# One decoder step on one core: prompt projections normalised in groups of four token tiles, rope tables built one stage earlier, and the two page loads of a quad issued apart

## Chip, cores and metric

The kernel runs on one core of one Trainium2 chip. The metric is device time in microseconds (us) from one launch to its end; the median of several executions is compared. A profile of one execution is used to see where the time goes.

Engines are named as the profile names them: PE (TensorE matmuls), PEld (its weight loads, which overlap the matmuls), DVE (VectorE), ACT (ScalarE), POOL (GpSimd) and SP (SyncE, whose queue issues nearly all DMAs here).

## The reference, cut to what matters

One decoder layer for two groups of requests with the same weights: a prompt of 1024 tokens and eight samples of four new tokens, each sample with 4096 past tokens kept in pages. The three sub-layers are a mixer, a cross-attention into 256 memory tokens and a gated ConvFFN. The mixer is what the change touches:

```
u, v, cq, ckv, kpe = split_in(rms_norm(x) @ w_in)        # 1024 -> 512 | 512 | 256 | 256 | 32
a_out = chunk_gmlp(u, v, ...)                            # group A, 512 wide
ckv_n = rms_norm(ckv)
q = qk_rope(rms_norm((rms_norm(cq) @ w_uq) as 8 heads x 96))
k = qk_rope(rms_norm(concat(ckv_n @ w_uk as 8 x 64, kpe broadcast to 8 heads x 32)))
v = ckv_n @ w_uv
b_out = causal softmax attention of q, k, v              # group B, 512 wide
mixed = concat(rms_norm(a_out), rms_norm(b_out)) @ w_o
```

For the samples the keys and values of the past are computed from the paged latents (`cache_ckv`, 256 wide) and un-rotated rope keys (`cache_kpe`, 32 wide) that `page_table` names. The RMS norm of each key head runs over its 64 projected and its 32 rope columns, and the rope half is rotated by position after the norm.

## The kernel before, in words

All matmuls work on float32 split into a high and a low part: `mm3` (line 179, its matmuls have line 185) issues three products for each pair of operands. Tokens are cut into nine tiles: eight of 128 prompt tokens and one of the 32 sample tokens. Outside the stretches named below a planner (`tc`, with a cost model) orders the instructions of every engine; inside `tc.manual_schedule(engines=...)` the named engines keep the order of the program text.

**Latents' stage** (end of `phase1`, lines 485 to 568). After u, v and the gMLP, the latents cq and ckv are projected in three chunks of up to 384 tokens. For each chunk ACT squares, PE sums over partitions, DVE computes the inverse root (`rsqrt_steps`, 11 small DVE instructions, lines 222 to 236) at high priority, and the normalised ckv is written out and split. Between the chunks `mix_group` (lines 1494 to 1522) normalises the group-A outputs in groups of two tiles (five groups), transposes them on PE (line 1519), copies them from PSUM on DVE (line 1520) and stores each tile with one DMA (line 1522) to a DRAM scratch `mix`.

**Prompt projections, first half of the heads** (`phase2a`, lines 597 to 650). Three small tables are loaded; POOL multiplies the cosines and sines with the rope gains for q and for k (`rope_tables`, line 591), squares and rotates the rope keys of all tiles (`kss`, `kr`). Then `proj_group` (line 797) runs for tiles in groups (0,2), (2,4), (4,6), (6,8) and (8,9). A group allocates its buffers (`k` and `q`, rings of four, two tiles each), projects q and k of each tile with copies and squares on ACT and a reduction on DVE (line 828), then calls `norm`: three small DVE instructions (lines 833 to 835), the 11 of the inverse root, one more (line 841), the rope of q on POOL (`rope_tok`, lines 579 to 582), and the scaling of k on DVE (line 850) and of the rope keys on POOL (line 851). The values follow. After the groups `head_prep` transposes q and k of head 0 (line 874) and the first scores begin.

**Heads** (lines 681 to 750). PE, ACT, DVE and POOL are in manual order: 32 units (head, group of two query tiles) in 80 steps of a counter `t`. Work of the second half of the heads is put on chosen steps by `spread`: the four prompt groups of `proj_group` on steps 16 to 20, 18 to 23, 21 to 26 and 24 to 29 (line 672), their values on 28 to 38. On POOL, sums of later weights (`weight_sums`, lines 772 to 776) run on every fourth step. When the outputs of a group of query tiles are complete, a `mix` (line 697) normalises them as above.

**Page loop** (`phase2b`, lines 1050 to 1164). Eight samples with 32 pages each; four pages make a quad, so there are 64 quads, and a step `n` of the loop scores two pages: 128 steps, two for a quad. For quad R two tiles are loaded, with four DMAs each: `cT` (the pages with the features on partitions, latents and rope keys: what the key scores are made from; ring of three, line 1220) and `ck` (the pages with the tokens on partitions, for the values and the sums of squares of the rope keys; ring of 15, line 1224). `quad_load` (line 1202) first brings four page numbers into registers of SP (line 1207: one TENSOR_LOAD and four register computations with range checks), then issues the DMAs. The first three `cT` are loaded during the heads (line 1043), their `ck` at steps -6, -4 and -2; from step 0 on each even step n calls `quad_load` once, for both tiles of quad n/2 + 3 (line 1121). `cT` of quad R is free for quad R + 3 when `quad_prep` has split it (POOL and DVE, line 1252, at step 2R - 1). At step 2R - 3 POOL rotates the rope keys of R (`quad_rot`, lines 1237 to 1239), at step 2R - 1 PE multiplies them (line 1267), and at 2R the scores proper start. `ck` of quad R is read at step 2R + 1 (ACT, line 1260) and by the value matmuls (line 1367) some 20 steps later. PE, ACT, DVE and POOL are in manual order; SP is the planner's, with a dependency (line 1211) that holds its register loads near the DMAs of five quads before. Other tiles pass through the ring of `ck` as well: the last prompt mix, four loads of mixed rows (line 1088, steps 20, 36, 52 and 68) and the first loads of the next stage (line 1130, from step 122).

**After the loop**: memory keys and values (`mem_kv`), output projection, memory attention, the FFN. The change does not touch these.

Of the kernel before, what the change touches and what calls it, by code (L numbers as in the profile page):

```python
# [5 lines left out]
F32 = mybir.dt.float32  # L6
# [148 lines left out]
class Net:  # L155
# [132 lines left out]
    def phase1(self):  # L288
# [198 lines left out]
        def mix(i0):  # L487
            hl = self.t(pl, [P, 2, 4, P], F32, "hl")
            hl = [hl[:, i] for i in range(2)]
            self.mix_group(pl, pp, 0, i0, min(i0 + 2, 9), lambda i: a_all[:, i], hl, lambda j: self.t(pl, [P, 512], F32, "csq", 4), ("st", 3))  # L490
# [17 lines left out]
        ck_tok = self.t(pl, [P, 9], F32, "ck_tok")  # L508
        raws = pl, [P, 512], F32, "uraw", 1
# [6 lines left out]
        for c, (o, n) in enumerate(CH):  # L516
# [50 lines left out]
            for i0 in ((0, 2), (4, 6), (8,))[c]:  # L567
                mix(i0)
# [15 lines left out]
    def rope_tables(self, p, cos, sin, g, name):  # L584

        nc = self.nc
        out = []
        for nm, t in (("c", cos), ("s", sin)):
            o = p[nm] if isinstance(p, dict) else self.t(p, [P, 9, 2, 16], F32, f"{name}_{nm}")
            for h in range(2):  # L590
                nc.gpsimd.tensor_tensor(
                    o[:, :, h], t, g[:, h * 16 : h * 16 + 16].unsqueeze(1).broadcast_to([P, 9, 16]), ALU.mult
                )
            out.append(o.rearrange("p i h d -> p i (h d)"))
        return out

    def phase2a(self):
# [3 lines left out]
        self.kr = self.t(p, [P, 9, 32], F32, "kr")  # L601
# [7 lines left out]
        pre = self.t(px, [P, 1024], F32, "pre", 2)  # L609
        cos, sin = (pre[:, a : a + 144].rearrange("p (i d) -> p i d", i=9) for a in (0, 144))  # L610
        grow = pre[:, 288:352]
        nc.sync.dma_start(cos, I["c_cos"])
        nc.sync.dma_start(sin, I["c_sin"])
        nc.sync.dma_start(grow, I["rows"][:, 1024:].partition_broadcast(P))
        qt = self.rope_tables(p, cos, sin, grow[:, :32], "tq")
        pre2 = self.t(px, [P, 1024], F32, "pre", 2)
        pre2 = {n: pre2[:, a : a + 288].rearrange("p (i h d) -> p i h d", i=9, h=2) for n, a in (("c", 0), ("s", 288))}
        kt = self.rope_tables(pre2, cos, sin, grow[:, 32:], "tk")
        cmraw = pre[:, 640:768]
# [13 lines left out]
        kss = self.t(p, [P, 9], F32, "kss")  # L633
        ksq = pre[:, 352:640].rearrange("p (i d) -> p i d", i=9)
        nc.gpsimd.tensor_tensor(ksq[:, :8], self.kpe[:, :8], self.kpe[:, :8], ALU.mult)
        nc.gpsimd.tensor_tensor(ksq[:NS, 8:], self.kpe[:NS, 8:], self.kpe[:NS, 8:], ALU.mult)
        nc.vector.tensor_reduce(kss[:, :8], ksq[:, :8], AX.X, ALU.add)
        nc.vector.tensor_reduce(kss[:NS, 8:], ksq[:NS, 8:], AX.X, ALU.add)
        for w, i0, i1 in ((P, 0, 8), (NS, 8, 9)):
            k4 = [x[:w, i0:i1].unsqueeze(2) for x in (self.kr, self.kpe)]  # L640
            self.rope_tok(p, k4[0], k4[1], [t[:w, i0:i1] for t in kt], 1, w, i1 - i0)

        rq = self.t(p, [P, 8, 8], F32, "rq")
        c = {"ggq": ggq, "cmask": cmask, "rq": rq, "kss": kss, "qt": qt}
# [30 lines left out]
        spread(sum([v for _, v in late], []) + late[4][0], 28, 38)  # L675
# [5 lines left out]
        with tc.manual_schedule(engines={E.PE, E.Activation, E.DVE, E.Pool}):  # L681
# [13 lines left out]
            hls = []  # L695

            def mix(G):
                yield
                if not hls:
                    hl = self.t(p, [P, 8, 4, 64], F32, "v", 2).rearrange("p a b c -> p (a b c)")  # L700
                    hls.extend(hl[:, a : a + 1024].rearrange("p (k n) -> p k n", k=4) for a in (1024, 0))
                hl = hls.pop()
                hl = [hl[:, :, a : a + P] for a in (0, P)]
                nt = lambda j: self.t(p, [P, 2, 4, 96], F32, "k", 4).rearrange("p m h d -> p (m h d)")[:, :512]
                for k, _ in enumerate(self.mix_steps(pm, pp, 1, 2 * G, 2 * G + 2, lambda i: self.b_all[G][:, i % 2], hl, nt, ("tp", 4))):
                    yield
                    if k:
                        yield

            mixes = {28: 0, 29: 2, 30: 1}  # L710
            wsums = dict(zip(range(22, 75, 4), (NK, NK + 1, *range(NK))))
            self.lows = []
            for n, u in enumerate(units):
                nu = units[n + 2] if n + 2 < len(units) else None
                k = u["n"]
                for j in range(k):
                    self.flush()
                    u["T"](j)
                    for f in outs:
                        f()  # L720
                        done += 1
                        if done in mixes:
                            steps.append(mix(mixes[done]))
# [73 lines left out]
    def proj_group(self, p, pp, hf, i0, i1, s, c, tt=("tp", 4)):  # L797
# [5 lines left out]
        def alloc():  # L803
            nonlocal r, kk, q
            r = self.t(p, [P, 2, 2, 4], F32, "hr", 2)[:tn, :m]
            kk = self.t(p, [P, 2, 4, 96], F32, "k", 4)[:tn, :m] if i0 < 8 else None
            q = self.t(p, [P, 2, 4, 96], F32, "q", 4)[:tn, :m] if i0 < 8 else self.qs[:, hf * 4 : hf * 4 + 4].unsqueeze(1)
# [22 lines left out]
        def norm():  # L830
# [14 lines left out]
            self.rope_tok(p, q[:, :, :, 64:], q[:, :, :, 64:], [t[:tn, i0:i1] for t in c["qt"]], 4, tn, m)  # L845
# [100 lines left out]
    def sample_prep(self, pp):  # L946
# [67 lines left out]
        nc.tensor.transpose(tp, self.kr[:NS, 8], self.ident[:NS, :NS])  # L1014
# [35 lines left out]
    def phase2b(self):  # L1050
# [27 lines left out]
        hl = self.t(p, [P, 4, 288], F32, "ck", 15).rearrange("p k n -> p (k n)")[:, :1024].rearrange("p (m k n) -> p m k n", m=2, k=4)  # L1078
        hl = [hl[:, i] for i in range(2)]
        mix = self.mix_steps(pa, ppt, 1, 6, 8, lambda i: self.b_last[:, i % 2], hl, None, ("m", 1))  # L1080
# [73 lines left out]
        with tc.manual_schedule(engines={E.PE, E.Activation, E.DVE, E.Pool}):  # L1154
            steps(-10, last + 1)
# [46 lines left out]
    def quad_load(self, p, Q, d=None):  # L1202
# [8 lines left out]
        if len(self.page_dma) >= 5:  # L1211
# [286 lines left out]
    def mix_steps(self, p, pp, z, i0, i1, src, hl, nt, tt):  # L1498
# [3 lines left out]
        r = self.t(p, [P, 2], F32, "mixr", 2)[:tn, :m]  # L1502
        ns = []
        for i in range(i0, i1):

            n = nt(i - i0)[:tn] if nt else src(i)[:tn]
            ns.append(n)
            o = n if nt else hl[i - i0][:tn].rearrange("p k n -> p (k n)")
            nc.scalar.activation(o, src(i)[:tn], AF.Square, accum_out=r[:, i - i0 : i - i0 + 1])
# [3 lines left out]
        for i, n in enumerate(ns):  # L1513
            nc.scalar.activation(n, src(i0 + i)[:tn], AF.Copy, scale=r[:, i : i + 1])
# [794 lines left out]
```

## Time and profile before

| | us |
|---|---|
| median of 3 runs | 1870.41 (1868.35 to 1872.27) |
| the profiled execution | 1873.17 |
| its span, first to last instruction | 1871.5 |
| PE busy in the span | 1812.4 (97%) |
| mean granted TensorE clock | 0.991 of full speed |

Stages of the profiled execution, read from the order of the instructions: latents and all before them to 185.3 us, prompt projections (first half) to 221.6, heads to 433.9, page loop to 886.2, the rest to 1871.5.

How to read it: a row of the windows view gives, for one stretch, its length and the busy time of PE, PEld, DVE, ACT and POOL with instruction counts, then the granted clock (1.00 is full speed, 0.50 half), the DMA share and GB/s. A row of the timeline or of a group gives start, duration, engine, line and operation; in square brackets stands how long the engine was idle before it and what ended that. "SPq" is SP's DMA queue: its rows are issues, not transfers.

### The profile page before, as it was taken

How to read it: one execution, taken by the hardware profiler on the slowest of the kernel's cores; microseconds unless marked ns; L12 is line 12 of the kernel's file. 1: busy time of each engine (PE TensorE's matmuls, PEld its weight loads, DVE VectorE, ACT ScalarE, POOL GpSimd, SP SyncE). 2: the span in 40 equal slices, each digit the busy share in tenths (PEclk: the TensorE clock that was granted, in tenths of full speed). 3: DMA queues.
4: the chain of work that ended last, by engine and by line, in shares of the span. 5: the costliest groups of instructions: out<-in, count | busy, mean ns of one | idle time of the engine just before them, and what ended most of it. 6: DMA issues, size and time to landing. Idle time of an engine off the chain costs nothing.

```text
span 1871.5 us, 39806 instructions
## 1 busy us (share of the span) xinstructions
PE 1812.4 (97%) x14402; PEld 1746.4 (93%) x14402; DVE 1382.2 (74%) x2883; ACT 928.9 (50%) x1965; POOL 708.0 (38%) x826
## 2 busy tenths in 40 slices
PE   6999899989999999999999999999999999999999
PEld 6999799889999999998799988899999999999999
DVE  6865967766887667776744676888888888878664
ACT  6435676666555655555533455633333333344442
POOL 1221515643535454443313110267776677500000
PEclk9999899999999999999999999999999999999999
DMA  8202204666776667564554345422222222495242
GB/s 286 70 10 68 82 1 165 222 230 175 219 205 186 180 173 200 162 186 128 182 157 134 135 158 154 129 67 81 81 82 90 69 72 77 113 352 167 78 154 76
DMA packets 139784, 260.18 MB, mean 139 GB/s; under 512 B 20546, under 2 KB 82851, under 8 KB 136515
## 3 DMA queue, kind: packets, MB, share of 16 engines
q1 hardware_dynamic: 138722, 256.58, 43.8%
q8 instruction: 114, 1.87, 0.4%
q10 hardware_dynamic: 864, 1.05, 0.2%
q14 instruction: 84, 0.68, 0.1%
HBM read 212.27 MB, written 45.30 MB: 138 GB/s over the span
## 4 chain that ended last, share of the span: by engine, by line
PE 61%; issue 5%; SPq 3%; DMA 3%; DVE 3%; POOL 2%; ACT 1%; POOLq 0%; DVEq 0%; ACTq 0%
PE d L185 12%; PE s L185 11%; PE b L185 7%; PE F L185 7%; PE X L185 6%; PE E L185 6%; PE A L185 3%; PE y L185 3%; DMA cT<-cT 2%; SPq L1220 2%; SPq L1224 1%; PE o L1367 1%; PE t L185 1%; POOL cl L1252 1%; PE v L185 1%
## 5 line engine op out<-in xcount | busy, mean ns | idle before, releaser
L185 PE MATMUL s<-w2h,ch 128*128 128x288 f32 (+1 forms) x1024 | 303.7, 297 | 0.0
L185 PE MATMUL s<-w2h,cl 128*128 128x288 f32 (+1 forms) x1024 | 296.0, 289 | 4.2 <-POOL cl L1252 3.0
L185 PE MATMUL s<-w2l,ch 128*128 128x288 f32 (+1 forms) x1024 | 294.6, 288 | 0.0
L185 PEld LDWEIGHTS s<-w2h,ch 128*128 128x128 f32 x1024 | 192.6, 188 | 8.3 <-ACT sq L1292 2.5
L185 PEld LDWEIGHTS s<-w2h,cl 128*128 128x128 f32 x1024 | 192.4, 188 | 6.5 <-POOL cl L1252 5.0
L185 PEld LDWEIGHTS s<-w2l,ch 128*128 128x128 f32 x1024 | 192.8, 188 | 0.0
L1295 DVE TENSOR_REDUCE ss<-sq 128x16 f32<-128x1024 f32 x128 | 155.3, 1213 | 32.4 <-ACT sq L1292 32.2
L1252 POOL TENSOR_TENSOR cl<-cT,ch 128x512 fp32r<-128x512 f32 x64 | 83.7, 1307 | 113.2 <-ACT ch L1248 92.5
L1292 ACT ACTIVATE sq<-s 128x512 f32<-128x512 f32 x128 | 76.6, 598 | 88.8 <-PE s L185 88.7
L1289 ACT ACTIVATE sq<-s 128x512 f32<-128x512 f32 x128 | 76.7, 600 | 74.5 <-PE s L185 74.0
L191 ACT CAST a<-brb 128x528 fp32r<-128x528 f32 x77 | 48.8, 634 | 111.4 <-PE d L185 107.9
L185 PE MATMUL mm<-whi,xh 128*128 128x256 f32 (+3 forms) x288 | 83.4, 291 | 16.4 <-ACT xh L195 10.0
L192 DVE TENSOR_TENSOR a<-brb,a 128x528 fp32r<-128x528 f32 x77 | 54.3, 707 | 58.3 <-ACT a L191 58.3
L185 PE MATMUL d<-a,w 128*128 128x264 f32 x768 | 95.4, 284 | 0.5 <-DVE G L2087 0.5
L185 PEld LDWEIGHTS d<-a,w 128*128 128x128 f32 x768 | 94.3, 188 | 0.7 <-issue 0.7
L932 PEld LDWEIGHTS o<-v,pth 128*128 128x128 f32 x576 | 75.7, 197 | 8.4 <-ACT pth L922 4.2
L185 PE MATMUL mm<-wlo,xh 128*128 128x256 f32 (+3 forms) x288 | 82.1, 288 | 0.0
L185 PE MATMUL mm<-whi,xl 128*128 128x256 f32 (+3 forms) x288 | 82.1, 289 | 0.0
L932 PE MATMUL o<-v,pth 128*128 128x64 f32 x576 | 76.3, 274 | 5.6 <-ACT pth L922 3.3
L1958 POOL TENSOR_TENSOR lo<-s,hi 128x1024 fp32r<-128x1024 f32 x20 | 62.9, 3142 | 45.7 <-ACT hi L1957 45.7
L1248 ACT CAST ch<-cT 128x512 fp32r<-128x512 f32 x128 | 73.4, 625 | 3.7 <-DMA cT<-cT 3.6
L2013 ACT COPY a<-A 128x264 f32<-128x264 f32 x43 | 16.1, 375 | 118.7 <-PE A L185 113.9
(725 smaller groups left out, 6447.5 us busy)
## 6 DMA issues: line engine op xcount, KB each, us to landing
cT<-cT SPq DMA_DIRECT2D x256, 160.0 KB, 2.8
ck<-ck SPq DMA_DIRECT2D x256, 144.0 KB, 3.4
raw<-w_up SPq DMA_DIRECT2D x44, 512.0 KB, 3.6
wsumd<-wsum SPq DMA_DIRECT2D x13, 1024.0 KB, 4.2
actd<-cv SPq DMA_DIRECT2D x44, 264.0 KB, 2.4
brb<-actd SPq DMA_DIRECT2D x44, 264.0 KB, 5.6
wsum<-w_down SPq DMA_DIRECT2D x11, 1024.0 KB, 5.0
raw<-wsumd SPq DMA_DIRECT2D x20, 512.0 KB, 3.7
```

Of the source, the lines that this page charges most:

```text
L185: self.nc.tensor.matmul(out, l, r, start=first and i == 0, stop=last and i == len(seq) - 1)
L191: {"act": nc.scalar.copy, "pool": nc.gpsimd.tensor_copy, "dve": nc.vector.tensor_copy}[eng](hi, src)
L192: low = lambda: nc.vector.tensor_tensor(lo, src, hi, ALU.subtract)
L932: nc.tensor.matmul(u["o"][:, e], th[:, z * P : z * P + P], s["v"][:, jj, h % 4], start=j == z == 0, stop=e == 1 and jj == 2 * G + 1)
L1220: dmas.append([nc.sync.dma_start(cT[:, j], I["cT"][bass.ds(rv, 1)].rearrange("a p n -> (a p) n")) for j, rv in enumerate(rvs)])
L1224: nc.sync.dma_start(ck[j * 32 : j * 32 + 32], I["ck"][bass.ds(rv, 1)].rearrange("a t s f -> (a t) s f"))
L1248: nc.scalar.copy(d["h"][:, k], src[k])
L1252: (nc.vector if k else nc.gpsimd).tensor_tensor(d["l"][:, k], src[k], d["h"][:, k], ALU.subtract)
L1289: nc.scalar.activation(sq[:, 0], ps[:, :, n0 : n0 + 256], AF.Square)
L1292: nc.scalar.activation(sq[:, 1], pt.rearrange("p (e d) -> p e d", e=2), AF.Square)
L1295: yield lambda: nc.vector.tensor_reduce(s["ss"][:, g0 : g0 + 2].rearrange("p e (z h) -> p z e h", z=2), sq.rearrange("p z e (h d) -> p z e ...
L1958: eng.tensor_tensor(lo, src, hi, ALU.subtract)
```

## The change

1. `mix_steps` works on groups of up to four tiles in the latents' stage ((0,4), (4,8), (8,9); the last two are both placed after the second chunk, none after the third). It normalises in place, puts two tiles side by side in one buffer and stores them with one DMA.
2. The rope tables of q, the squares `kss` and the rotated keys `kr` are made in the latents' stage (`rope_setup`, new) instead of at the start of `phase2a`: three DMAs, 16 POOL and 2 DVE instructions there, in place of 18 POOL and 2 DVE instructions.
3. `proj_group` runs for groups (0,4), (4,8), (8,9), with buffers of four tiles in rings of two. In the first half the parts of the groups are interleaved by hand; in the second half the two prompt groups go to steps 16 to 23 and 21 to 29. The rope of four tiles is done two tiles at a time.
4. The prompt mixes in the heads use a buffer of the `k` or `q` ring and have one more step between their two tiles.
5. In the page loop SP joins the manual order. On even steps `quad_load` is called twice: for `cT` of quad n/2 + 3, then for `ck` of quad n/2 + 2. The `ck` of quads 0, 1 and 2 are issued at steps -6, 0 and 1. The dependency of line 1211 is kept for the first three quads alone.

```diff
-            for i0 in ((0, 2), (4, 6), (8,))[c]:
+            for i0 in ((0,), (4, 8), ())[c]:
                 mix(i0)
...
+        self.rope_setup(pl, lat)
...
-        groups = ((0, 2), (2, 4), (4, 6), (6, 8), (8, 9))
-        for g in groups:
-            for f in sum(self.proj_group(p, pp, 0, *g, st[0], c, ("mm", 5)), []):
-                f()
+        groups = ((0, 4), (4, 8), (8, 9))
+        gs = [self.proj_group(p, pp, 0, *g, st[0], c, ("mm", 5)) for g in groups]
+        (qk, v), (qk1, v1), (qk2, _) = gs
+        for f in qk + v + qk1[:5] + v1[:2] + qk1[5:9] + qk2[:3] + qk1[9:] + v1[2:] + qk2[3:]:
+            f()
...
-        for (q, _), t in zip(late, ((16, 20), (18, 23), (21, 26), (24, 29))):
+        for (q, _), t in zip(late, ((16, 23), (21, 29))):
             spread(q, *t)
...
-            kk = self.t(p, [P, 2, 4, 96], F32, "k", 4)[:tn, :m] if i0 < 8 else None
+            kk = self.t(p, [P, 4, 4, 96], F32, "k", 2) if i0 < 8 else None
...
-                if n % 2 == 0 and 0 <= Q + AHEAD < NB * 8:
-                    quads[Q + AHEAD] = self.quad_load(p, Q + AHEAD, quads.get(Q + AHEAD))
+                if n == -6:
+                    self.quad_load(p, 0, quads[0])
+                if n >= 0 and n % 2 == 0 and Q + AHEAD < NB * 8:
+                    quads[Q + AHEAD] = self.quad_load(None, Q + AHEAD)
+                if n == 0:
+                    self.quad_load(p, 1, quads[1])
+                if (n == 1 or n > 0 and n % 2 == 0) and Q + 2 < NB * 8:
+                    self.quad_load(p, Q + 2, quads[Q + 2])
...
-        with tc.manual_schedule(engines={E.PE, E.Activation, E.DVE, E.Pool}):
+        with tc.manual_schedule(engines={E.PE, E.Activation, E.DVE, E.Pool, E.SP}):
             steps(-10, last + 1)
...
-        if len(self.page_dma) >= 5:
+        if p is None and new and len(self.page_dma) >= 5 and Q < 3:
...
         for i, n in enumerate(ns):
+            if i % 2 == 0:
+                hl, w = new(i // 2), min(2, m - i) * tn
             tp = self.t(pp, [P, 512], F32, *tt).rearrange("p (k n) -> p k n", k=4)[:, :, :tn]
             for k in range(4):
                 nc.tensor.transpose(tp[:, k], n[:, k * P : k * P + P], self.ident[:tn, :tn])
-            nc.vector.tensor_copy(hl[i][:, :, :tn], tp)
-            o = t0 + i * tn
-            nc.sync.dma_start(self.mix_dram[:, z * 4 : z * 4 + 4, o : o + tn], hl[i][:, :, :tn])
-            if nt is None and i < m - 1:
+            nc.vector.tensor_copy(hl[:, :, i % 2 * tn : i % 2 * tn + tn], tp)
+            if i % 2 or i == m - 1:
+                o = t0 + i // 2 * 2 * tn
+                nc.sync.dma_start(self.mix_dram[:, z * 4 : z * 4 + 4, o : o + w], hl[:, :, :w])
+            elif z:
                 yield
```

The new function, without its loads:

```python
    def rope_setup(self, p, lat):
        ...
        for nm, t in (("c", cos), ("s", sin)):
            o = self.t(lat, [P, 9, 2, 16], F32, f"tq_{nm}")
            for h in range(2):
                nc.gpsimd.tensor_tensor(o[:, :, h], t, grow[:, h * 16 : h * 16 + 16].unsqueeze(1).broadcast_to([P, 9, 16]), ALU.mult)
        ...
        for w, i0, i1 in ((P, 0, 8), (NS, 8, 9)):
            m = i1 - i0
            x, kr = (y[:w, i0:i1] for y in (self.kpe, self.kr))
            sq = self.t(p, [P, 512], F32, "csq", 4)[:w, : m * 32].rearrange("p (i d) -> p i d", i=m)
            nc.gpsimd.tensor_tensor(sq, x, x, ALU.mult)
            nc.vector.tensor_reduce(self.kss[:w, i0:i1], sq, AX.X, ALU.add)
            nc.gpsimd.tensor_tensor(kr, x, grow[:w, 32:].unsqueeze(1).broadcast_to([w, m, 32]), ALU.mult)
            ...
            for z, y in enumerate((cos, sin)):
                nc.gpsimd.tensor_tensor(t[:, z], ...)
            nc.gpsimd.tensor_tensor(kr[:, :, :16], t[:, 0, :, 0], t[:, 1, :, 1], ALU.subtract)
            nc.gpsimd.tensor_tensor(kr[:, :, 16:], t[:, 0, :, 1], t[:, 1, :, 0], ALU.add)
```

More of the change, by code (lines that the diff above doesn't have):

```diff
@@ L608, in phase2a @@
         st = [{**heads(), **self.wqv}]
[L609 to L619, printed above, removed]
+        cmraw = self.t(px, [P, P], F32, "cmraw")
         nc.sync.dma_start(cmraw, I["c_causal"])
@@ L693, in sample, with mix @@
                 yield from self.pages_ahead()
-            hls = []
-            def mix(G):
+            def mix(G, ring):
                 yield
[L699 to L705, printed above, removed]
+                n = self.t(p, [P, 4, 4, 96], F32, ring, 2).rearrange("p m h d -> p (m h d)")
+                hl = n[:, 512:].rearrange("p (k n) -> p k n", k=4)
+                for k, _ in enumerate(self.mix_steps(
+                    pm, pp, 1, 2 * G, 2 * G + 2, lambda i: self.b_all[G][:, i % 2], lambda j: hl, lambda j: n[:, :512], ("tp", 4)
+                )):
                     yield
```

79 lines of the change are left out of this document (42 added, 37 removed).

## The prediction

> **What bounds the kernel now.** I read the stage table first (the windows view cut at the order of the instructions), because the busy share of the page (PE 97%) is an average.
>
> ```profile
> PE 1812.4 (97%) x14402; PEld 1746.4 (93%) x14402; DVE 1382.2 (74%) x2883; ACT 928.9 (50%) x1965; POOL 708.0 (38%) x826
> ```
> ```profile
> 0.00:185.30 185.30, 168.87 (x1257) 164.73 (x1258) 124.00 (x407) 89.80 (x187) 37.94 (x50) 0.99 0.32 107
> 185.30:221.60 36.30, 28.05 (x203) 25.95 (x203) 35.17 (x128) 24.99 (x122) 24.34 (x47) 0.94 0.39 119
> 221.60:433.90 212.30, 201.01 (x1486) 188.45 (x1485) 147.22 (x510) 144.08 (x385) 86.59 (x92) 0.95 0.40 142
> 433.90:886.20 452.30, 446.98 (x3700) 422.10 (x3702) 335.43 (x641) 261.13 (x572) 209.04 (x339) 1.00 0.65 184
> 886.20:1871.50 985.30, 967.50 (x7766) 945.15 (x7763) 740.39 (x1202) 408.85 (x702) 350.10 (x299) 1.00 0.38 124
> ```
>
> The reader is to see that PE is the bound in all stages but one. In the prompt projections (185.3 to 221.6) it is busy 28.05 of 36.30 us, idle 8.25, and DVE is busy 35.17: there DVE ends last. In the page loop PE is idle 5.3 of 452.3 us: nothing can be won there, only lost. Next, the clock in shorter windows, and PE's timeline at the end of the projections:
>
> ```profile
> 217.60:221.30 3.70, 0.55 (x4) 0.12 (x1) 3.70 (x21) 1.27 (x2) 1.13 (x1) 0.50 0.01 2
> 221.30:227.80 6.50, 6.21 (x21) 5.18 (x22) 5.96 (x25) 2.66 (x7) 0.00 (x0) 0.50 0.00 0
> 309.80:316.60 6.80, 6.76 (x29) 6.73 (x30) 3.23 (x11) 0.95 (x2) 6.41 (x7) 0.50 0.55 230
> ```
> ```profile
> 210.09 0.28 PE L185 MATMUL mm<-wvh,ckh 128*128 128x256 f32 x1
> ...
> 213.13 0.28 PE L185 MATMUL mm<-w2h,ckl 128*32 128x256 f32 x1
> ...
> 216.91 1.25 PE L874 MATMUL tp<-ident,q 128*96 128x128 f32 x8
> ...
> 221.33 0.66 PE L874 MATMUL tp<-ident,k 128*96 128x128 f32 x2 [3.17 <-DVE rqa L234]
> 221.64 0.46 PE L185 MATMUL s<-kTh,qTh 96*128 96x128 f32 x1
> ```
>
> The last projection starts at 213.13, the first score at 221.64. Between them PE waits for the norm of the last group on DVE. The wait costs twice: from 217.6 to 227.8 the clock is granted at half, and the 6.8 us of matmuls in it (0.55 + 6.21) would take half as long, 3.4 us less. The same follows a gap in the heads (309.8 to 316.6).
>
> **Prompt projections: -5.** The rows of DVE by form, 186 to 223 us, and the norm of tile 8's mix in the timeline:
>
> ```profile
> L850 DVE TENSOR_TENSOR k<-k,hr 128x512 f32<-128x512 f32 x4 | 3.7, 916 | 0.0
> L834 DVE TENSOR_TENSOR hr<-hr,sq_tok 128x8 f32<-128x8 f32 x4 | 2.0, 501 | 0.1
> ...
> L236 DVE SCALAR_TENSOR_TENSOR rqy<-rqh,rqy 128x16 f32<-128x16 f32 x4 | 0.7, 169 | 0.0
> ```
> ```profile
> 188.61 0.13 DVE L222 TENSOR_SCALAR rqx<-mixr 32x1 f32<-32x1 f32 x1
> ...
> 193.13 0.30 DVE L236 SCALAR_TENSOR_TENSOR mixr<-rqh,rqy 32x1 f32<-32x1 f32 x1
> ```
>
> A norm is 15 small instructions and L850. The 60 small ones of the four prompt groups (13 rows, L834 to L236) sum to 16.6 us; with two groups half go, 8.3 us, since their length hardly depends on the width. L850 keeps its elements. Tile 8's mix norm (188.6 to 193.4, 11 instructions, 3.4 us) goes ahead of the third chunk, and so out of the way of that chunk's inverse root. DVE's 35.2 us fall to about 23; PE's 28 become the bound, and behind them stands the tail of the last norm. Of PE's 28.05 us the values of two tiles and the sample tile (210.09 to 213.4, 3.3) come after tile 7's keys in the new order, and so do head 0's transposes (some 2, the row at 216.91 among them). So tile 7's keys can leave PE at 185.3 + 28.05 - 5.3 = 208.0 and be squared and reduced by 209.5 (1.5 is my allowance). Then 15 instructions at 0.28 (16.6/60) take 4.2, L850 at twice the width 1.8, the last transposes and copies 1: scores at 216.5 in place of 221.6, **-5**. Ends: 0 (the norm of four tiles starts only with its last tile, and this waits as late as before) and -11.7 (all 8.25 us of idle and the 3.4 of half clock go).
>
> The Trainium skill ("TensorE: Matmul & The Clock Gate", What's actually happening) lets the clock halve after an idle window of about 3.4 us. Here 3.17 us of waiting were enough, so a tail of 2 us may still be charged; by the page it would not be, and the sum would be 3.4 lower.
>
> **Rope tables and mixes of the latents' stage: 0.** 16 POOL and 2 DVE instructions and three DMAs move to before 185.3, where POOL is busy 38 of 185 us and DVE 124: PE hides them. Two inverse roots fewer and five stores in place of nine there are off PE's path too. If the cover fails (the new scratch comes from the ring of the squares, so ACT's first square of a chunk could wait for POOL), it costs some us once; 0 to +2.
>
> **Heads: -1.** The gap and what DVE did before it:
>
> ```profile
> 309.84 0.69 PE L185 MATMUL s<-kTh,qTh 96*128 96x384 f32 x1 [2.08 <-DVE pr L905]
> ```
> ```profile
> 301.94 1.14 DVE L224 TENSOR_SCALAR rqy<-rqy 128x16 int32<-128x16 int32 x1
> ...
> 307.17 1.57 DVE L850 TENSOR_TENSOR k<-k,hr 128x512 f32<-128x512 f32 x1
> ```
>
> A late norm beside POOL's weight sums takes 5 us and holds the scores' DVE work. Two norms in place of four are two chances fewer, but L850 is then twice as wide in one piece (3 us at this row). At best the gap goes with its half clock (2.08 + 6.76/2 = 5.5), at worst another comes (+4). I take -1, nearest to nothing. The mixes' extra step moves one transposition behind the last unit: nothing is late by it.
>
> **Page loop: +9.5.** `quad_load` is called twice for a quad, so its register loads are issued twice. What one set costs is seen in SP's timeline, where a set lies between some groups of four DMAs and not between others; all else that I need stands here too:
>
> ```profile
> L1207 SPq TENSOR_LOAD <-pages x67: 293/298/1196, 367.1 to 848.5; - x67
> ```
> ```profile
> 435.88 8.32 SPq L1224 DMA_DIRECT2D ck<-ck  x12
> 445.85 1.93 SPq L1220 DMA_DIRECT2D cT<-cT  x4
> ...
> 451.93 1.93 SPq L1220 DMA_DIRECT2D cT<-cT  x4
> ...
> 519.63 1.92 SPq L1220 DMA_DIRECT2D cT<-cT  x4
> 521.80 1.85 SPq L1224 DMA_DIRECT2D ck<-ck  x4
> 525.36 2.73 SPq L1220 DMA_DIRECT2D cT<-cT  x4
> 529.72 1.85 SPq L1224 DMA_DIRECT2D ck<-ck  x4
> ...
> 857.14 1.92 SPq L1220 DMA_DIRECT2D cT<-cT  x4
> 859.32 1.85 SPq L1224 DMA_DIRECT2D ck<-ck  x4
> 861.27 0.36 SPq L1130 DMA_DIRECT2D ck<-w_mk  x1
> 873.39 0.83 SPq L1130 DMA_DIRECT2D ck<-memT  x2
> ```
> ```profile
> 458.58 0.47 PE s L1267 x2
> ...
> 623.64 3.00 PE s L185 x22
> ...
> 851.98 3.01 PE s L185 x22
> ...
> 877.14 9.01 PE s L185 x72
> ```
>
> 67 sets are 64 and 3 for the quads loaded in two calls; afterwards there are 128. From `cT` to `ck` without a set SP rests 0.25 us (519.63 + 1.92 to 521.80); with one, 1.63 (525.36 + 2.73 to 529.72); from `ck` to `cT` with one, 1.71. So a quad costs SP 1.92 + 0.25 + 1.85 + 1.71 = 5.73 us now and 1.92 + 1.63 + 1.85 + 1.71 = **7.11** afterwards. PE needs a quad every (851.98 - 623.64)/32 = 7.14 us. SP, which has a fifth of its time to spare today, has none left: every delay of it stays.
>
> Its schedule afterwards: `ck` of quad 0 at 435.9, `cT` of 3 at 439.4 (now 445.85), then `ck` of 1 and 2 with their sets, so `cT` of 4 at 450.0 (now 451.93), and `cT` of 63 at 450.0 + 59 x 7.11 = 869.5, plus 3.4 for the seven single DMAs that now stand in the same order: 872.9, now 857.14. From the first issue of a `cT` to its use PE needed 458.58 - 451.93 = 6.65 us, so step 125 starts at 879.6 in place of 877.14: +2.4. To this comes what lengthens SP's issues. In the 49 groups of each kind from 519.63 to 859.32 they took 18.7 us more than 1.92 and 1.85 a group, 0.38 for a quad, much of it where eight DMAs follow each other closely. They will be spread evenly, four in 3.55 us; I take a third of it, 0.12: 59 x 0.12 = 7.1. **+9.5.** Ends: +24.8 (0.38 stays) and -4 (what PE now waits in the loop for `cT`'s followers, row below; more can't be won). Who waits: `cT` issues stand behind `ck` issues and these behind `cT` buffers; POOL's rotation waits for `cT`, PE's rope product for POOL. In favour of the change is that `cT` no longer stands behind a `ck` that waits for the value matmuls (16.7 us), but SP had the time.
>
> ```profile
> PE s L185 <- POOL cl L1252: 3.0, 8, 0.7
> ```
> ```profile
> SPq L1224 <- PE o L1367: 16.7, 5, 5.2
> ```
>
> The Trainium skill ("DMA: Bandwidth & Descriptors", Latency and other measured facts) gives a floor of about 600 ns for a tensor load. The row says 298 ns, and that is used; by the page two sets would take 0.6 us more and the loop 36 us more.
>
> **End of the loop: +1.5.** The first loads of the next stage are queued on SP behind the last `ck`: now at 861 and 873, afterwards some 10 us behind `cT` of 63, so at 882 to 886. They then land near the loop's end, and the first memory keys may wait: 0 (they still come in time) to +4 (a few us of transfer are bare); I take a value nearer to nothing.
>
> **Sum.** -5 - 1 + 9.5 + 1.5 = +5.0. The profiled execution took 1873.2 (span 1871.5, 1.7 around it), 2.8 above the median of 1870.4; the sum is set on the median: **1875.4 us, slower**.
>
> **The rivals.**
>
> (a) *SP keeps up*: sets overlap with something or buffers leave slack, the loop costs 0 to 2.4. Then -6 + 1.2 + 0 = about 1865.5; with the prompt gap gone altogether 1859. For it: SP's need and PE's differ by only 0.03 us a quad. Against it: extra single DMAs and any stretch. It decides below a stretch of 0.04. Faster. 0.28.
>
> (b) *SP's issues stay as long as now*: the loop +24.8, end +2, prompt -6: 1891. For it: the group at 525.36 follows a rest of 1.7 us and still is 0.8 longer than 1.92, so close issues can't be all of it. 0.17.
>
> (c) *The prompt stage wins nothing*: the tail of a four-tile norm takes the place of the old one, the loop as forecast: 1880. DVE's 35.17 of 36.30 us speaks against it. 0.10.
>
> (d) *All small*: the change does in neither place what it says; 1870, within the bound. 0.05.
>
> **Chances.** Forecast 0.40 (its own range 1871 to 1881). 0.2% of 1870.4 is 3.7 us, about what a measurement of this kernel can tell from no change: 1866.7 to 1874.1 is "same". Faster: most of (a), 0.25. Same: the rest of (a), (d), and the lower part of the forecast, 0.20. Slower: 0.55. The range from 1861 to 1892 leaves out the tails of (a) and (b).
>
> **What would show it.** Right: 128 sets at L1207; SP's queue in the loop without rests, 7.1 to 7.4 us a quad; POOL's rotation waiting for `cT` and PE for it; `cT` of 63 issued some 12 to 25 us later relative to the loop's start; the first score 4 to 6 us earlier, DVE no longer full before it. Wrong: SP resting within the quads, batches of eight quads still 57 us; or the first score no earlier than 220; or a new gap with half clock in the heads.

## The result and the profile after

The changed kernel takes **1896.66 us** (1894.77 to 1899.23), the kernel before 1871.32 (1868.35 to 1872.27) beside it: ratio 1.0137, 95% interval 1.0124 to 1.0150. The forecast of 1875.4 had the sign, not the size, and its range ended at 1892.

The profiled execution has a span of 1893.8 us, 22.3 more than before. First the page of the changed kernel, its row of busy times and its chain of work:

```profile
PE 1820.6 (96%) x14402; PEld 1751.0 (92%) x14402; DVE 1370.3 (72%) x2797; ACT 929.7 (49%) x1965; POOL 703.5 (37%) x821
...
PE 72%; SPq 7%; DMA 6%; DVE 5%; issue 4%; ACT 3%; POOL 3%; DVEq 0%; POOLq 0%; ACTq 0%
```

PE's work is nearly the same. In the chain SP's queue and the DMAs, 3% each before, now have 7 and 6%. Where in the program is told by the product of the rotated keys (`bd`, `krq`), two matmuls at the head of each of the 64 quads; one row each from the view of that line, before and after (count, shortest, median and longest duration in ns, then first and last start):

```profile
L1267 PE MATMUL s<-bd,krq x128: 270/273/377, 433.7 to 876.9; 128*128 128x128 f32 x128
```
```profile
L1277 PE MATMUL s<-bd,krq x128: 270/275/377, 428.8 to 899.7; 128*128 128x128 f32 x128
```

By the first of the two matmuls of a quad, which the row doesn't tell from the second, the starts are 433.75 and 876.76, afterwards 428.76 and 899.59. So the stages stand as follows (before, after): first score 221.64, 218.18 (-3.5); heads 212.1, 210.6 (-1.5); loop from first to last product 443.0, 470.8 (**+27.8**); the rest 994.7, 994.2 (-0.5). The sum is +22.3. By stage, the windows view of the changed kernel (columns PE, PEld, DVE, ACT, POOL, then clock, DMA share, GB/s):

```profile
185.30:218.18 32.88, 27.73 (x198) 26.01 (x197) 24.97 (x91) 23.66 (x116) 16.08 (x27) 0.92 0.39 130
218.18:428.76 210.58, 199.22 (x1484) 187.03 (x1484) 136.48 (x470) 144.45 (x385) 87.55 (x91) 0.96 0.39 140
428.76:899.59 470.83, 446.06 (x3623) 416.31 (x3622) 336.24 (x621) 256.06 (x561) 200.23 (x334) 1.00 0.61 173
899.59:1893.80 994.21, 976.65 (x7842) 954.67 (x7840) 748.58 (x1219) 414.23 (x712) 352.68 (x305) 1.00 0.39 126
```

In the loop PE now idles 24.8 us of 470.8. Who waits, in the loop (us in total, times, longest; the first fence is of before, the next three of the changed kernel):

```profile
POOL krq L1237 <- DMA cT<-cT: 32.2, 10, 4.6
```
```profile
POOL krq L1247 <- DMA cT<-cT: 239.0, 58, 6.5
```
```profile
PE s L1277 <- POOL ck L1150: 12.2, 15, 2.2
PE s L1277 <- POOL krq L1249: 5.4, 6, 1.5
```
```profile
SPq L1230 <- POOL cl L1262: 1.8, 6, 0.4
SPq L1234 <- PE o L1377: 1.6, 6, 0.3
```

POOL's rotation waits for `cT` in 58 of 64 quads (10 before), PE for POOL (L1150 is a short memset that POOL does right behind the rotation), and SP, at the head of this chain, for hardly anything: its longest waits for the page loop's compute are in the fourth fence. Before, between 520 and 880 us alone, it waited 16.7 us for `o` (the row in the prediction) and 18.1 for `cl`:

```profile
SPq L1220 <- POOL cl L1252: 18.1, 10, 2.5
```

SP is simply never done. Its queue, from the timeline (start, length, DMAs of the group):

```profile
446.42 2.29 SPq L1230 DMA_DIRECT2D cT<-cT  x4
...
484.77 1.91 SPq L1230 DMA_DIRECT2D cT<-cT  x4
488.25 1.84 SPq L1234 DMA_DIRECT2D ck<-ck  x4
492.13 2.23 SPq L1230 DMA_DIRECT2D cT<-cT  x4
495.94 1.84 SPq L1234 DMA_DIRECT2D ck<-ck  x4
499.48 1.92 SPq L1230 DMA_DIRECT2D cT<-cT  x4
502.97 1.84 SPq L1234 DMA_DIRECT2D ck<-ck  x4
504.92 0.36 SPq L1134 DMA_DIRECT2D fold<-c_fold  x1
506.98 3.13 SPq L1230 DMA_DIRECT2D cT<-cT  x4
...
892.02 2.89 SPq L1230 DMA_DIRECT2D cT<-cT  x4
...
902.29 0.36 SPq L1140 DMA_DIRECT2D ck<-w_mk  x1
```
```profile
L1217 SPq TENSOR_LOAD <-pages x128: 293/299/993, 362.5 to 898.4; - x128
```

There are 128 sets as foreseen. From `cT` of quad 4 (446.42) to that of quad 63 (892.02) SP takes 445.6 us, **7.55 us a quad**, where 7.11 was the sum of its parts and PE needs 7.14. Batches of eight quads take 59 to 62 us in place of 57.

### The profile page after: what moved, and what is told of

Its sections match the earlier page's. It is cut to its first block, busy times and chain, and to the rows that moved or that the text cites. A ratio compares the mean times of both kernels' runs of the same rounds, so it can differ in the third digit from the quotient of the medians.

```text
span 1893.8 us, 40238 instructions
## 1 busy us (share of the span) xinstructions
PE 1820.6 (96%) x14402; PEld 1751.0 (92%) x14402; DVE 1370.3 (72%) x2797; ACT 929.7 (49%) x1965; POOL 703.5 (37%) x821
## 4 chain that ended last, share of the span: by engine, by line
PE 72%; SPq 7%; DMA 6%; DVE 5%; issue 4%; ACT 3%; POOL 3%; DVEq 0%; POOLq 0%; ACTq 0%
PE d L185 12%; PE s L185 9%; PE mm L185 8%; PE b L185 7%; PE X L185 7%; PE F L185 7%; PE E L185 7%; PE A L185 3%; SPq L1230 3%; PE y L185 3%; PE o L936 3%; SPq L1217 2%; DMA cT<-cT 2%; SPq L1234 2%; DMA ck<-ck 1%
## 5 line engine op out<-in xcount | busy, mean ns | idle before, releaser
L1247 POOL TENSOR_TENSOR krq<-cT,cosT 128x128 f32<-128x128 f32 x64 | 30.4, 475 | 239.1 <-DMA cT<-cT 239.0
L1301 DVE TENSOR_TENSOR S<-s,S 128x64 f32<-128x64 f32 x128 | 28.2, 220 | 79.0 <-ACT sq L1299 78.9
```

## The experiments

The theory: SP's instructions set the pace of the loop, because each quad has a second register set of 1.4 us; the new places of the issues cost nothing. The rival: the written order of SP's queue costs, each issue standing behind others that wait.

**e1, one set a quad.** The order of the issues is kept; the values are loaded once.

```diff
-        ld, rvs = nc.values_load_multi_w_load_instructions(...)
+        ld, rvs = [], d.pop("rvs", None)
+        if rvs is None:
+            ld, rvs = nc.values_load_multi_w_load_instructions(...)
+        if p is None and Q >= 3:
+            d["rvs"] = rvs
```

> The changed kernel, but the registers that a quad's set loaded for its cT issues are kept for its ck issues two steps later, so a quad has one set again (about 67 TENSOR_LOAD in place of 128); the hand order of SP and everything else stays. Theory (SP's queue is the bound because of the second set): a quad costs SP 7.55 - 1.4 = about 6.15 us, below PE's 7.14, so batches of eight quads take 57 us again, the loop 443 us from first to last rope product, the total about 1867 (1863 to 1870), faster than before by the 5.0 us that the first rope product comes earlier (428.8 in place of 433.8). Rival A (the hand order of SP costs: cT behind ck, ck behind buffers): the order is untouched, so batches stay near 60 us and the total at 1890 to 1897. Rival B (both): in between, 1875 to 1885.

1867.29 us, ratio to before 0.9978 (0.9968 to 0.9987). The loop of e1 and its SP queue:

```profile
L1281 PE MATMUL s<-bd,krq x128: 270/273/377, 432.1 to 874.0; 128*128 128x128 f32 x128
```
```profile
480.08 1.91 SPq L1234 DMA_DIRECT2D cT<-cT  x4
482.17 1.84 SPq L1238 DMA_DIRECT2D ck<-ck  x4
485.71 1.92 SPq L1234 DMA_DIRECT2D cT<-cT  x4
487.82 1.84 SPq L1238 DMA_DIRECT2D ck<-ck  x4
491.36 1.92 SPq L1234 DMA_DIRECT2D cT<-cT  x4
```

SP needs 5.63 us for a quad here (480.08 to 485.71), the loop takes 441.8 us, and batches take 57 from the third on. Only the set was taken out, and 29 us of loop went with it. The rival falls.

**e6, two short sets.** Both sets stay, without the range check of the values.

```diff
             self.pages[0:1, Q * 4 : Q * 4 + 4], engines=[mybir.EngineType.SP], min_val=0, max_val=319,
+            skip_runtime_bounds_check_because="...",
```

> The changed kernel with both sets of a quad, but without the range check of the page numbers, so that of a set only the TENSOR_LOAD stays (0.30 us and 0.05 between, in place of 1.4); the numbers are the same, nothing is computed otherwise. Theory: a quad costs SP 7.55 - 2 x 1.05 = 5.45 us, below PE's 7.14, so batches of 57 us and a total like that with one set, 1867.3 (1863 to 1870). Rival (the number of loads of registers counts, not their instructions): 1885 or more.

1866.32 us, 0.9969 (0.9959 to 0.9978), loop 440.6. The row of the sets in e6:

```profile
L1217 SPq TENSOR_LOAD <-pages x128: 293/299/501, 364.0 to 858.4; - x128
```

128 loads again, and no loss: it is the time of the set on SP that counts, over 1 us of which is the eight instructions of the check.

**e5, three sets.** The other way: one more, unused, for each quad.

```diff
+        if p and Q >= 3:
+            nc.values_load_multi_w_load_instructions(...)
```

> The changed kernel with a third register set for each quad from the fourth on, right ahead of the set of its ck issues; nothing uses its values. Theory (SP's instructions set the pace, so each microsecond more on SP is one more on PE): a quad takes 7.55 + 1.4 = 8.95 us, batches of eight 71 to 72 us, and 60 quads at 1.42 more make 1896.7 + 85 = about 1982 (1972 to 1990). Rival A (the changed order of the issues or their landing sets the pace, and the sets lie beside it): under 1930.

1973.67 us, ratio 1.0546 (1.0519 to 1.0574); the loop is 541.3 us, batches take 69 to 72 from the second on. Two quads of its SP queue, undisturbed:

```profile
541.04 1.85 SPq L1238 DMA_DIRECT2D ck<-ck  x4
544.59 1.92 SPq L1234 DMA_DIRECT2D cT<-cT  x4
549.50 1.86 SPq L1238 DMA_DIRECT2D ck<-ck  x4
```

A quad takes 8.46 us (541.04 to 549.50), 1.4 more than the 7.03 of such a quad in the changed kernel and the 7.11 of the sum. Over the whole loop (`cT` of quad 4 at 447.90, of 63 at 965.21) SP's quad goes from 7.55 to 8.77 only, 1.22 more; the missing 0.18 is accounted for below. From one set to three the loop is 441.8, 470.8, 541.3: flat while SP is faster than PE, and SP's own time from there.

**e4, the second set in the old order.** Before, with an unused set for each quad, no DMA written elsewhere.

```diff
+        if new and p:
+            nc.values_load_multi_w_load_instructions(...)
```

> The kernel before, in its own order of issues, with a second register set for each quad from the fourth on whose values nothing uses (61 TENSOR_LOAD more with their checks); no DMA is moved. Theory (instructions on SP): a quad costs SP 5.73 + 1.4 + 0.4 = about 7.5 us, over PE's 7.14, so batches take about 60 us and the total is 1890 to 1900, though no issue changed its place. Rival A (the order costs, not the sets): 1870 to 1874, batches of 57 us.

1888.14 us, 1.0090 (1.0073 to 1.0107). The expectation of 1890 to 1900 was missed by 2 us, and the trace tells why: here SP's order is the scheduler's, which drew the unused sets forward. 32 sets lie ahead of the loop (5 before), and in its batches 12, 17, 17, 16, 12, 11, 7 and 4. Those with 16 or 17 take 61.1, 62.6 and 59.3 us, the later ones 57.8, 56.9 and 57.2. The order of the issues is the old one, and the loss comes and goes with the sets.

**e3 and e2, the halves of the change.** e3 is before with the new page loads alone; e2 is the changed kernel with the old ones.

```diff
-                if n % 2 == 0 and 0 <= Q + AHEAD < NB * 8:
-                    quads[Q + AHEAD] = self.quad_load(p, Q + AHEAD, quads.get(Q + AHEAD))
+                if n >= 0 and n % 2 == 0 and Q + AHEAD < NB * 8:
+                    quads[Q + AHEAD] = self.quad_load(None, Q + AHEAD)
+                ...
+                if (n == 1 or n > 0 and n % 2 == 0) and Q + 2 < NB * 8:
+                    self.quad_load(p, Q + 2, quads[Q + 2])
```

> The kernel before with the new page loads alone (two calls and two sets a quad, SP in hand order). Theory: the loop alone costs its 27.8 us (470.8 us from first to last rope product in the changed kernel, 443.0 before), so 1870.4 + 27 = about 1898 (1893 to 1902). Rival (the loss needs both parts, since the loop starts earlier in the changed kernel than its loads): 1880 to 1890.

> The changed kernel with the page loads of before (one call and one set a quad, SP not in the hand order of the loop): the prompt groups, the rope tables and the mixes alone. Theory: the whole loss is in the page loop, so this is faster than before by what the prompt stage and the heads gained, 5.0 us in the trace of the changed kernel: about 1866 (1863 to 1870), batches of 57 us. Rival (something of the first stages disturbs the loop too, as by buffers or by the order in which its loads start): batches over 58 us, 1872 or more.

e3: 1898.09 us, 1.0139 (1.0120 to 1.0159). e2: 1868.04, 0.9986 (0.9976 to 0.9997), 2.6 us faster with 0.5 to 4.5 in the interval, less than the 5.0 of the single trace. The loop of e3 takes 466.5 us, 23.5 more than before. The new page loads explain the loss alone.

**e9, the rope part alone.** Before, with the rope tables and rotated keys made in the latents' stage; groups of two, old mixes, old page loads.

```diff
+        self.rope_setup(pl, lat)
...
-        qt = self.rope_tables(p, cos, sin, grow[:, :32], "tq")
...
-        kt = self.rope_tables(pre2, cos, sin, grow[:, 32:], "tk")
```

> The kernel before with only the rope tables and the rotated keys moved into the latents' stage; groups of two, mixes and page loads as before. Three profiles of the old prompt stage have their first score at 220.3 to 221.6, the ones of the new stage at 217.8 to 219.2. Theory (the wider groups halve the norms' small instructions and so give the gain; the moved instructions lie beside other work in either place): first score 220 to 222, total 1869 to 1873. Rival (what is moved was in the way on DVE and POOL): first score 217.5 to 219.5, total 1867 to 1869.

1867.29 us, 0.9984 (0.9974 to 0.9995); its first score is at 217.12. The theory fell. The stage from the first projection to the first score in three kernels: before, changed, e9 (columns as above):

```profile
185.25:221.64 36.39, 28.14 (x204) 26.04 (x203) 35.27 (x128) 25.04 (x122) 24.34 (x47) 0.94 0.39 119
```
```profile
184.38:218.18 33.80, 28.65 (x204) 26.93 (x203) 25.89 (x93) 24.28 (x117) 16.77 (x28) 0.92 0.39 131
```
```profile
184.94:217.11 32.17, 27.22 (x204) 25.87 (x203) 30.18 (x126) 25.30 (x122) 16.78 (x30) 1.00 0.40 129
```

The moved work takes 7.6 us from POOL (24.34 to 16.78). From DVE it takes 5.1 (35.27 to 30.18), though only two of DVE's instructions went, 0.56 us. The rest is in the length of the others. More than half of that lies in the inverse root's instructions (lines 222 to 236): in before they take 0.35 us on average where a POOL instruction runs beside them (31 of 71) and 0.165 where none does; in e9 16 of 71 have one beside them. One step of the same norm, in before beside the rope tables on POOL, in e9 beside nothing on POOL:

```profile
190.06 0.42 DVE L235 SCALAR_TENSOR_TENSOR rqh<-rqa 32x1 f32<-32x1 f32 x1
```
```profile
189.44 0.15 DVE L235 SCALAR_TENSOR_TENSOR rqh<-rqa 32x1 f32<-32x1 f32 x1
```

The stage is 32.2 us long with the rope part alone, 33.8 with everything. The groups of four take 4.3 us more from DVE, and yet the stage is 1.6 us longer with them. That repeats: 32.2 in both profiles with the rope part and no groups of four (e9, e12), 33.8 in all five with the changed kernel's stage (changed, e1, e2, e5, e6), 35.7 to 36.4 in the three of the old one.

**e7, no interleaving by hand** (on e1).

```diff
-        for f in qk + v + qk1[:5] + v1[:2] + qk1[5:9] + qk2[:3] + qk1[9:] + v1[2:] + qk2[3:]:
+        for f in sum(sum(map(list, gs), []), []):
```

> One set as in e1, and the three prompt groups of four tiles issued one after the other, without the interleaving by hand of the second group's values and the sample tile behind tile 7's keys. Theory: the prompt stage ends with the norm of the last group of four; interleaved, 3 us of PE's work stands behind it, so without it the first score comes 2 to 4 us later (218.2 and 219.0 in the two traces with interleaving; 220 to 223 here) and the total is 1869 to 1872. Rival (the scheduler orders the stage itself, so the written order matters little): first score 217.5 to 219.5, total within 1.5 of e1.

1864.85 us, 0.9966 (0.9952 to 0.9981), first score 219.18, as with it. That part of the rival holds, but not its reason: PE does follow the written order (in e1 the sample tile ends at 209.1 and values follow, in e7 values come first and the sample tile ends at 211.4). In both some 3 to 4 us of PE's work stand behind tile 7's keys, which leave PE at 207.4 and 207.5, so the norm of these starts no sooner. The total is 2.4 below e1, where the rival allowed 1.5, and the two intervals overlap.

**e8, the second half's weight splits later** (on e1).

```diff
-        st.append({**heads(), **self.proj_weights((pm, [P, 512], F32, "pth", 5), 1)})
+        st.append(heads())
...
+        extra[3].append(lambda: st[1].update(self.proj_weights((pm, [P, 512], F32, "pth", 5), 1)))
```

> One set as in e1, and the loading and splitting of the second half's weights (4 splits on DVE, 1.9 us between the steps of the last prompt norm in the changed kernel's trace, 210.1 to 212.8) is moved behind the first units of the heads. Theory: the last norm of four tiles ends some 1 to 2 us earlier, the first score comes at 216.5 to 217.5, and the total is 1 to 2 us below e1, unless the splits hold the scores there. Rival (POOL's product for the keys, 2.1 us from 213.3, and the squares on ACT set the end): first score unchanged within 0.5 us.

1864.10 us, 0.9965 (0.9946 to 0.9985), first score 217.12, 0.7 to 2.1 earlier than in the six traces of groups of four with the splits there; the stage is 32.7 us long, 1.1 less than with them. Against e1 the total differs by less than the intervals.

**e10, e11, what the new order is worth with one set.** e10 joins e1, e7 and e8; e11 is e10 with the old page loads.

> One set a quad, the prompt groups one after the other (e7) and the second half's weight splits behind the first units of the heads (e8). Theory: the two small edits add up as far as the last norm is still what ends the prompt stage: first score 216.5 to 217.5, batches of 57 us, total 1863 (1860.5 to 1866). Rival (each of the two differences from e1 was scatter between runs): 1866 to 1868.

> As e10, with the page loads of before (one call a quad, SP not in the hand order). It tells what the new order of the page loads is worth once its second set is gone. Theory: nothing or little, since PE waited only 4.1 us in the whole loop before: within 2 us of e10. Rival (the loop's first batch gains: 48 to 50 us in four profiles of the new order without the long second set, 53.4 in e2): 2 to 4 us above e10.

e10: **1863.68 us**, 0.9964 (0.9951 to 0.9977). e11: 1867.92, 0.9982 (0.9973 to 0.9991). The rival of e11 held, its theory didn't: the difference is 4.2 us, though the two intervals overlap by a little. PE's waits in the loop of e11 have a row that e10's haven't:

```profile
PE s L1272 <- POOL krq L1244: 3.0, 1, 3.0
```

In e11 `cT` of quad 3 is issued 12.6 us after the first product, behind `ck`s, in e10 after 5.9. The first batch takes 54.7 and 50.1 us. The profile of e11 is of the slowest of its executions (1874.95 us). Two more pairs differ in the page loads alone: e1 is 0.8 us below e2, and e12 (next) 1.4 below e9, or 2.8 by their ratios to before. From first to last product the loop is 4.6, 3.3 and 2.0 us shorter in the three pairs. So the new order wins something in the loop, and in the total between 1 and 4 us; how much isn't settled.

**e12, the two parts that count.** e9 with the new page loads and one set; no groups of four.

> The kernel before with two things alone: the rope tables and rotated keys in the latents' stage (e9) and the new order of the page loads with one register set a quad (as in e1). Prompt groups, late groups and mixes are those of before. Theory (the groups of four bring nothing; the moved rope work brings the prompt stage's gain and the order of the issues the loop's first batch): first score 217 to 218, first batch of the loop 48 to 50 us, then 55.5 and 57, total 1862 to 1866, as e10. Rival (the groups of four are worth something behind the prompt stage, in the heads): 1867 to 1870.

1865.93 us, 0.9969 (0.9956 to 0.9983), first score 217.17, first batch 49.8. Its interval overlaps that of e10, which has the groups of four: in the total these bring nothing that can be measured.

## Why the prediction was wrong, point by point

**Page loop, +9.5; measured +27.8. This is the step that failed, in the size of one term.** The mechanism was as told: 128 sets, SP without rests, POOL waiting on `cT`, PE on POOL, and a quad without a delay takes SP 7.03 us (495.94 to 502.97) where 7.11 was worked out. What failed is "much of it where eight DMAs follow each other closely. They will be spread evenly ... I take a third of it, 0.12". The delay was 7.55 - 7.11 = 0.44, of which the seven single DMAs, counted apart, make 0.06. The 0.38 that before showed stayed whole: 26 page issues are over 0.45 us long in the loop of before, 19.7 us too much together, and 26 in that of the changed kernel, 18.0 us, though the issues are spread evenly now. The working even held the counter-evidence, in rival (b): the long group at 525.36 that followed a rest. The 0.32 more a quad (7.55 against 7.11 + 0.12) over 59 quads are 18.9 us, less the 3.4 of the single DMAs 15.5. 1.4 more come from the start of the sequence (`cT` of quad 4 is 17.7 us behind the first product, foreseen 16.3) and 0.9 from the way from issue to use (892.02 to 899.59, 7.57 in place of 6.65). Together 17.8 of the miss of 18.3. Rival (b), +24.8 at a chance of 0.17, named the right case, and its 1891 still lay 5.7 us below the measured time.

Where the 0.38 comes from can be read in the instructions of SP. From 445 to 895 us 46 intervals are over 0.1 us longer than the median of their kind, 23.1 us together. 21 of them stand 128 SP instructions apart, 0.31 us each, 6.5 us: 0.11 a quad; behind 20 of these 21 an 8 KB block of code starts to load 1.0 to 2.0 us later. The other 25, 16.6 us, are single DMA issues of 0.5 to 1.7 us where the median is 0.34: 0.28 a quad. What lies beside them is seen in the DMA view of the two `cT` groups at 506.98 (3.13 us) and 499.48 (1.92 us), with packets, MB and the share of the time of 16 DMA engines for each queue:

```profile
q1 hardware_dynamic: 292, 0.32, 36.4%
q8 instruction: 1, 0.02, 2.8%
q14 instruction: 1, 0.01, 0.6%
```
```profile
q1 hardware_dynamic: 220, 0.26, 45.6%
```

During the long group blocks of code are loaded, one of 16 KB and one of 8 KB; during the short one none. In the loops of all fourteen profiles (both kernels and the twelve runs) 324 page issues are over 0.45 us, and 320 of them overlap such a block by over 50 ns; of the 6661 of usual length 533 do. In the changed kernel's own case a 16 KB block runs from 507.76 to 509.22 and an issue from 508.04 to 509.60. So the long issues go with the loading of code, and not with how closely SP's DMAs follow. In e5 there are 11 of them instead of 26, the excess is 7.7 us instead of 18.0, 0.18 a quad less: the missing part. Why so few is open, since SP's issues at their usual length take 30% of its longer loop and 35% of the changed kernel's. All this is a coincidence in time, very regular; that the block holds the issue was not tested by itself.

**Prompt projections, -5; measured -3.5 in the profile**, and -2.2 between the means of the profiles of the old stage (before, e3, e4: 220.8) and of the new one (changed, e1, e2, e5, e6: 218.6). By the length of the stage, from the first projection to the first score, it is -2.6 in the profile (36.4 to 33.8) and -2.2 between the means; the other 0.9 of the -3.5 is an earlier start (184.38 in place of 185.25). The sign held, and so did "DVE ends last" for before: DVE is busy 35.27 of the stage's 36.39 us. The reason for the gain failed. It was put down to fewer small instructions of the norms, at a mean of 0.28 us; e9 shows the whole gain with all of them in place. What filled DVE was their length beside the rope work on POOL: 0.35 us with POOL beside them, 0.165 without. POOL's work moved together with three small loads and two instructions of DVE, and no run takes these apart; nor was a kernel run with groups of four and the rope work left where it was. That the wider groups don't add to it is seen in the tail, in the timeline of the changed kernel:

```profile
213.29 1.22 DVE L854 TENSOR_TENSOR k<-k,hr 128x1024 f32<-128x1024 f32 x1
```
```profile
213.31 2.10 POOL L855 TENSOR_TENSOR k<-kr,hr 128x512 f32<-128x512 f32 x1 [4.84 <-DVE rqa L234]
```
```profile
215.47 1.09 PE L878 MATMUL tp<-ident,k 128*96 128x128 f32 x4 [3.14 <-DVE rqh L235]
```

The sum had 1.8 us for DVE's product at twice the width (it is 1.22) and nothing for POOL's, which is twice as wide too: 2.10 us, ending at 215.41, 0.06 ahead of the transposes. The wait is named after DVE, but DVE's product ended at 214.51; the named instruction belongs to the sample tile. Ahead of it the splits of e8 lie between the norm's steps.

**Rope tables and mixes, 0.** Right for the place they went to: the projections start at 184.4 to 185.3 in the three profiles without the moved work and at 184.1 to 185.6 in the eleven with it. What they left was missed: this zero was the part with the gain.

**Heads, -1; measured -1.5**, but the heads take 209.4 to 213.8 us in the twelve experiments, and with the same code in them, but for the first page issues, 209.4 (e9) and 213.3 (e12). The term is below what one profile tells.

**End of the loop, +1.5; measured -0.5.** The first loads of the next stage came at 902, behind the last product, and the rest did not get longer. Hidden, the lower end of its bounds.

**The rivals.** (a) *SP keeps up* is what e1 and e6 made true: 1867.3 and 1866.3 where it gave 1865.5. (c) and (d) fell. The tensor load in the Trainium skill ("DMA: Bandwidth & Descriptors", Latency and other measured facts), about 600 ns, would by estimate have made two sets 0.6 us longer; the row after says 299 ns at the median, and 7.55 us is accounted for with that.

**The clock.** The prediction took the wait of 3.17 us for the cause of the half clock in before ("3.17 us of waiting were enough"). By its own rows that wait starts at 218.16, behind the transposes of 216.91, while the half clock starts at 217.6; in the 3.4 us ahead of 217.6 PE was busy for 1.54. It was right that the shorter tail would still be charged: the half clock lasts 10.2 us in the changed kernel too, from 213.1.

**What the prediction did not see** is that the new order can win some us once the second set is gone (4.2 between e10 and e11, less in the other two pairs): its floor of -4 came from what PE waits for, and was used as an end of the range only.

## What to carry to other kernels

A queue that issues DMAs is an engine with a cycle: sum its instructions for one turn, register loads and checks included, and compare with the turn of the engine that it feeds; at 7.11 against 7.14 us there is no room for anything. A delay that is measured per turn is kept whole until a row shows what it depends on. And where one engine is full, ask not only how many instructions it has but how long they are beside another engine's work: here taking that work away shortened the stage, and wider norms on top of it did not.

## What the runs showed of the hardware

A register set of four page numbers takes SP about 1.4 us, of which the load is 0.30 and the eight instructions of the range check about 1.03; without them two sets a quad cost nothing (e6).

SP loses 0.31 us at each 128th instruction, in every profile here. The Trainium skill ("Runtime: NRT & Kernel Launch", Instruction fetch mechanics) says that engines refill in blocks of 16 KiB, at a cost mostly hidden. In the changed kernel 114 blocks are of that size (q8 in the rows below; by their number they are PE's, whose 14402 matmuls and 14402 weight loads make some 250 for each) and 86 are of 8 KB (q14). On a queue that is the bound the cost isn't hidden: the halts at each 128th instruction make 0.11 us a quad, the long issues beside blocks 0.28, both tied to the blocks by their times alone:

```profile
q8 instruction: 114, 1.87, 0.4%
...
q14 instruction: 86, 0.70, 0.1%
```

Half clock comes in steps. Around the end of the heads it lasts 6.8 us in the changed kernel, 10.2 in before and 13.7 in e1, multiples of 3.4 us, and the heads take 210.6, 212.1 and 213.1 us: it may be a part of why they scatter. The Trainium skill ("TensorE: Matmul & The Clock Gate", What's actually happening) has a window of 3413 ns that runs freely; the steps agree with it. What starts them is not one long wait: in the changed kernel half clock begins at 213.1, and in the 3.4 us ahead of it PE had the 0.6 us of the transposes at 211.71, between a wait of 2.01 and the first part of one of 3.14; in before it was the 1.54 named above. The windows view there (PE's busy time first, clock third from the end):

```profile
209.70:211.70 2.00, 0.01 (x1) 0.02 (x1) 2.00 (x11) 2.00 (x13) 0.00 (x0) 1.00 1.02 414
211.70:215.40 3.70, 0.61 (x4) 0.37 (x4) 3.70 (x15) 1.06 (x3) 2.09 (x1) 0.69 0.30 121
215.40:218.20 2.80, 2.73 (x13) 2.29 (x13) 2.55 (x11) 1.26 (x2) 0.01 (x1) 0.50 0.00 0
```
